# The first store of a rotary-embedding kernel in two requests: 16 partitions, then 112

## The chip, the cores and the metric

The kernel runs on one core of a Trainium2 chip. The time is device microseconds of that core. Before the change it is 318.33 us, the median of three runs (318.25 to 318.38).

The core has engines with instruction streams of their own: VectorE (DVE), GpSimd (POOL), ScalarE (ACT), SyncE (SP) and TensorE (PE, not used here). Sixteen DMA engines move data between the chip's memory (HBM) and the on-chip memory (SBUF, 128 partitions). An engine's instruction stream asks for a transfer, and the DMA engines carry it out; SP's requests and ACT's requests stand in two queues, which the page calls q1 and q10.

## The reference

Rotary position embedding on `x` of shape (8, 2048, 16, 64): batch, position, head, element. The tables `cos` and `sin` have 32 columns for each position.

```
x1 = x[..., :32];  x2 = x[..., 32:]
out1 = x1 * cos - x2 * sin
out2 = x1 * sin + x2 * cos
out  = concatenate([out1, out2], axis=-1)
```

All is float32. The input and the output have 67.1 MB each.

## The kernel before

The 2048 positions of a batch lie on 128 partitions, 16 positions (J) on each. A piece is half of that, 8 positions (R) of one batch, so there are 16 pieces. A piece is 4 MB: 128 partitions with one contiguous run of 32 KB each, in SBUF as in HBM.

The buffer `buf` holds five pieces (NBUF). Piece p is loaded into slot p mod 5 by SP (`load`, line 52), is rotated in place, and is stored from there by ACT (`store`, line 55). The load of piece p + 5 is asked for after the store of piece p and has to wait until that store has landed. The loads of the first five pieces are asked for at the start, that of piece 0 in three parts with the two tables between them. The sixteen pieces make 18 loads of `x`, and, since the last piece is stored in three parts, 18 stores.

`rotate` (line 69) works on some of a piece's positions. VectorE multiplies the halves, swapped, by a sine table with its sign folded in, into a scratch tile `v` (line 80), and then multiplies the piece by the cosine table in place (line 93). GpSimd adds `v` (line 99). Most pieces take two such steps of four positions. In the last piece VectorE does part of the addition itself (lines 87 and 96). ScalarE prepares the tables (lines 108 to 110) and from then on only asks for stores.

The order of VectorE's instructions is fixed by `in_order`. For the rest, each engine follows the program's order, and the tile framework sets the waits: a store waits for the additions of its piece, a load for the store that frees its slot. The framework also gives each transfer one of eight semaphores, in turn; a transfer that takes over a semaphore waits until the transfer that had it before has landed.

The change touches `store` (line 54) and the branch for the first piece in the main loop (line 112), where the whole of piece 0 is stored with one request after three steps of `rotate`.

Of the kernel before, what the change touches and what calls it, by code (L numbers as in the profile page):

```python
# [1 line left out]

# [4 lines left out]


@with_exitstack  # L10
def kernel(
    ctx: ExitStack,
    tc: tile.TileContext,
    x: bass.AP,
    cos: bass.AP,
    sin: bass.AP,
    out: bass.AP,
):
    nc = tc.nc
    f32 = mybir.dt.float32  # L20

    B, S, H, D = x.shape
    Dh = D // 2
    P = nc.NUM_PARTITIONS
    J = S // P
    R = 8
    C = 4
    HALVES = J // R
    NP = B * HALVES
    NBUF = 5  # L30

    const_pool = ctx.enter_context(tc.tile_pool(name="rope_const", bufs=1))
    io_pool = ctx.enter_context(tc.tile_pool(name="rope_io", bufs=1))
    tmp_pool = ctx.enter_context(tc.tile_pool(name="rope_tmp", bufs=2))
    ps_pool = ctx.enter_context(tc.tile_pool(name="rope_ps", bufs=1, space=bass.MemoryType.PSUM))
    psv_pool = ctx.enter_context(tc.tile_pool(name="rope_psv", bufs=1, space=bass.MemoryType.PSUM))

    sin_f = const_pool.tile([P, J, Dh], f32)
    cos_f = const_pool.tile([P, J, Dh], f32)
    sin_p = ps_pool.tile([P, J, D], f32)  # L40
    cos_p = ps_pool.tile([P, J, Dh], f32)
    buf = io_pool.tile([P, NBUF, R, H, D], f32)

    def rows(t, p, r0, r1):
        b, j0 = p // HALVES, (p % HALVES) * R
        return t[b].rearrange("(p j) h d -> p j (h d)", j=J)[:, j0 + r0 : j0 + r1, :].rearrange("p j f -> p (j f)")

    def flat(t):
        return t.rearrange("p j h d -> p (j h d)")

    def load(p, r0=0, r1=R):
        nc.sync.dma_start(out=flat(buf[:, p % NBUF, r0:r1, :, :]), in_=rows(x, p, r0, r1))  # L52

    def store(p, r0=0, r1=R):
        nc.scalar.dma_start(out=rows(out, p, r0, r1), in_=flat(buf[:, p % NBUF, r0:r1, :, :]))

    order = []

    def in_order(op):
        if order:  # L60
            tc.add_manual_dep(
                op.ins,
                order[-1].ins.name,
                mybir.DependencyInfo(mybir.DependencyClass.NoSync, mybir.DependencyReason.DATA),
                reason="order of the vector engine",
            )
        order.append(op)

    def rotate(p, r0, r1, on_vector=0):
        n = r1 - r0  # L70
        j0 = (p % HALVES) * R + r0
        js = slice(j0, j0 + n)
        xt = buf[:, p % NBUF, r0:r1, :, :]
        rev = xt.rearrange("p j h (e d) -> p j h e d", e=2)[:, :, :, ::-1, :]
        sin_b = sin_p[:, js, :].rearrange("p j (e d) -> p j e d", e=2).unsqueeze(2).to_broadcast([P, n, H, 2, Dh])
        cos_b = cos_p[:, js, :].unsqueeze(2).to_broadcast([P, n, 2 * H, Dh])
        m = n - on_vector
        if m:
            v = tmp_pool.tile([P, C, H, D], f32)
            in_order(nc.vector.tensor_mul(  # L80
                out=v[:, 0:m, :, :].rearrange("p j h (e d) -> p j h e d", e=2),
                in0=rev[:, 0:m, :, :, :],
                in1=sin_b[:, 0:m, :, :, :],
            ))
        if on_vector:
            w = psv_pool.tile([P, 2, H, D], f32)
            in_order(nc.vector.tensor_mul(  # L87
                out=w[:, 0:on_vector, :, :].rearrange("p j h (e d) -> p j h e d", e=2),
                in0=rev[:, m:n, :, :, :],
                in1=sin_b[:, m:n, :, :, :],  # L90
            ))
        xw = xt.rearrange("p j h (e d) -> p j (h e) d", d=Dh)
        in_order(nc.vector.tensor_mul(out=xw, in0=xw, in1=cos_b))  # L93
        if on_vector:
            xa = flat(xt[:, m:n, :, :])
            in_order(nc.vector.tensor_add(out=xa, in0=xa, in1=flat(w[:, 0:on_vector, :, :])))  # L96
        if m:
            xa = flat(xt[:, 0:m, :, :])
            nc.gpsimd.tensor_add(out=xa, in0=xa, in1=flat(v[:, 0:m, :, :]))  # L99

    nc.sync.dma_start(out=sin_f, in_=sin.rearrange("(p j) d -> p j d", j=J))  # L101
    load(0, 0, 2)
    nc.sync.dma_start(out=cos_f, in_=cos.rearrange("(p j) d -> p j d", j=J))
    load(0, 2, 4)
    load(0, 4, R)
    for p in range(1, NBUF):
        load(p)
    nc.scalar.copy(out=sin_p[:, :, Dh:D], in_=sin_f)  # L108
    nc.scalar.mul(out=sin_p[:, :, 0:Dh], in_=sin_f, mul=-1.0)  # L109
    nc.scalar.copy(out=cos_p, in_=cos_f)  # L110
    for p in range(NP):
        if p == 0:
            rotate(p, 0, 2)
            rotate(p, 2, 4)
            rotate(p, 4, 8)
            store(p)
        elif p == NP - 1:
            rotate(p, 0, 4, 1)
            store(p, 0, 4)
            rotate(p, 4, 6, 1)  # L120
            store(p, 4, 6)
            rotate(p, 6, 8, 2)
            store(p, 6, 8)
        else:
            rotate(p, 0, 4)
            rotate(p, 4, 8)
            store(p)
        if p + NBUF < NP:
            load(p + NBUF)


# [1 line left out]
_INS = ['x', 'cos', 'sin']  # L133
_OUTS = [((8, 2048, 16, 64), 'float32')]


# [23 lines left out]
```

## Time and profile before

The table is of one profiled execution.

| What | Value |
|---|---|
| time of the profiled execution | 318.49 us |
| span of its instructions and transfers | 316.7 us |
| median of the runs | 318.33 us |
| GpSimd's additions (line 99) | 33, of which 29 on 128x4096 at 8.86 us |
| VectorE's products (lines 80 and 93) | 67, of which 59 on 128x4096 at 4.42 us |
| whole loads and stores of 4 MB | 15 each, median 31.4 us from request to landing |
| first store | asked for at 33.31 us, landed 24.0 us later |
| last arithmetic instruction ends | 306.2 us |

Times are counted from the start of the span. The time of an execution holds 1.8 us around the span. A duration from request to landing holds the time that a transfer stands in its queue behind others. The DMA rows of a profile give, for a stretch of time, the packets and bytes of each queue and the share of 16 engines' time that they took; a packet here is one partition's contiguous run, or a small packet that closes a transfer on an engine.

### The profile page before, as it was taken

To read this page: it belongs to the slowest core of one execution; us is meant where nothing else is said; L and a number is where in the kernel's file an instruction comes from. 1 tells how busy PE (TensorE), PEld (TensorE's weight loads), DVE (VectorE), ACT (ScalarE), POOL (GpSimd) and SP (SyncE) were. 2 spreads that over 40 slices of the span, in tenths; PEclk is the share of its full clock that TensorE was granted. 3 is DMA by queue.
4 is the path that set the end of the run, shared out by engine and by line. 5 is a ranking of instruction groups with operands and counts; after the bars stand their busy time and mean duration, and the time that the engine had idled before them with its cause. 6 is when DMAs were issued, how large, how long until landed. Compare 5 with 4: busy or idle time off the path is not lost.

```text
span 316.7 us, 272 instructions
## 1 busy us (share of the span) xinstructions
DVE 287.5 (91%) x73; ACT 3.1 (1%) x4; POOL 274.8 (87%) x37
## 2 busy tenths in 40 slices
DVE  2999999999999999999999999799697997979960
ACT  3000000000000000000000000000000000000000
POOL 0659999999999999999999999989969899797900
DMA  7999999999999999999999999999999999999997
GB/s 301 460 430 447 348 464 426 435 451 410 459 401 464 397 464 397 464 414 447 435 426 459 401 464 397 464 398 459 410 451 435 426 451 410 455 406 460 406 428 300
DMA packets 5474, 134.76 MB, mean 425 GB/s; under 512 B 608, under 2 KB 608, under 8 KB 864
## 3 DMA queue, kind: packets, MB, share of 16 engines
q1 hardware_dynamic: 2880, 67.63, 50.0%
q10 hardware_dynamic: 2592, 67.11, 49.1%
q14 instruction: 2, 0.02, 0.0%
HBM read 67.63 MB, written 67.11 MB: 425 GB/s over the span
## 4 chain that ended last, share of the span: by engine, by line
POOL 39%; DMA 32%; DVE 21%; issue 3%; SPq 0%; POOLq 0%; DVEq 0%
POOL buf L99 39%; DMA buf<-in_x_dram 22%; DMA out_dram<-buf 11%; DVE buf L93 10%; DVE v L80 8%; DVE buf L96 1%; DVE w L87 1%; SPq L101 0%; POOLq L99 0%; DVEq L80 0%; SPq L52 0%
## 5 line engine op out<-in xcount | busy, mean ns | idle before, releaser
L99 POOL TENSOR_TENSOR buf<-buf,v 128x4096 f32<-128x4096 f32 (+3 forms) x33 | 274.6, 8335 | 26.2 <-DVE buf L93 25.8
L80 DVE TENSOR_TENSOR v<-buf,sin_p 128x4096 f32<-128x4096 f32 (+3 forms) x33 | 137.3, 4161 | 17.3 <-DMA buf<-in_x_dram 15.7
L93 DVE TENSOR_TENSOR buf<-buf,cos_p 128x4096 f32<-128x4096 f32 (+1 forms) x34 | 141.8, 4170 | 1.2
L96 DVE TENSOR_TENSOR buf<-buf,w 128x1024 f32<-128x1024 f32 (+1 forms) x3 | 4.7, 1575 | 0.1
L87 DVE TENSOR_TENSOR w<-buf,sin_p 128x1024 f32<-128x1024 f32 (+1 forms) x3 | 4.7, 1579 | 0.0
L108 ACT ACT_TABLE_LOAD x1 | 1.3, 1283 | 0.7 <-PEq L144 0.7
L110 ACT COPY cos_p<-cos_f 128x512 f32<-128x512 f32 x1 | 0.6, 590 | 2.1 <-DMA cos_f<-in_cos_dram 2.1
L108 ACT COPY sin_p<-sin_f 128x512 f32<-128x512 f32 x1 | 0.6, 589 | 1.4 <-DMA sin_f<-in_sin_dram 1.4
L109 ACT ACTIVATE sin_p<-sin_f 128x512 f32<-128x512 f32 x1 | 0.6, 601 | 0.0
L144 POOL MEMSET const-float32-0.0<- 128x1 f32 x1 | 0.1, 98 | 0.2 <-issue 0.2
L144 POOL MEMSET const-bfloat16-1.0<- 128x1 bf16 x1 | 0.1, 101 | 0.0
L144 POOL MEMSET const-uint8-127<- 128x1 uint8 x1 | 0.1, 101 | 0.0
L144 POOL MEMSET const-float32-1.0<- 128x1 f32 x1 | 0.1, 98 | 0.0
## 6 DMA issues: line engine op xcount, KB each, us to landing
buf<-in_x_dram SPq DMA_DIRECT2D x15, 4096.0 KB, 31.4
out_dram<-buf ACTq DMA_DIRECT2D x15, 4096.0 KB, 31.4
buf<-in_x_dram SPq DMA_DIRECT2D x2, 1024.0 KB, 6.0
buf<-in_x_dram SPq DMA_DIRECT2D x1, 2048.0 KB, 11.5
out_dram<-buf ACTq DMA_DIRECT2D x1, 2048.0 KB, 11.9
out_dram<-buf ACTq DMA_DIRECT2D x2, 1024.0 KB, 10.8
sin_f<-in_sin_dram SPq DMA_DIRECT2D x1, 256.0 KB, 2.7
cos_f<-in_cos_dram SPq DMA_DIRECT2D x1, 256.0 KB, 5.1
```

The lines of the kernel that those rows point to most:

```text
L80: in_order(nc.vector.tensor_mul(out=v[:, 0:m, :, :].rearrange("p j h (e d) -> p j h e d", e=2), in0=rev[:, 0:m, :, :, :], in1=sin_b[:, 0:m ...
L87: in_order(nc.vector.tensor_mul(out=w[:, 0:on_vector, :, :].rearrange("p j h (e d) -> p j h e d", e=2), in0=rev[:, m:n, :, :, :], in1=sin_ ...
L93: in_order(nc.vector.tensor_mul(out=xw, in0=xw, in1=cos_b))
L96: in_order(nc.vector.tensor_add(out=xa, in0=xa, in1=flat(w[:, 0:on_vector, :, :])))
L99: nc.gpsimd.tensor_add(out=xa, in0=xa, in1=flat(v[:, 0:m, :, :]))
L108: nc.scalar.copy(out=sin_p[:, :, Dh:D], in_=sin_f)
L109: nc.scalar.mul(out=sin_p[:, :, 0:Dh], in_=sin_f, mul=-1.0)
L110: nc.scalar.copy(out=cos_p, in_=cos_f)
L144: nc = _bacc.Bacc("TRN2", target_bir_lowering=False, num_devices=1)
```

## The change

`store` gets a range of partitions, all 128 unless told otherwise, and the store of the first piece becomes two requests. The first has partitions 0 to 15, the second, directly behind it in ACT's stream, partitions 16 to 127. Both have all eight positions, 32 KB for each partition: 0.52 MB and 3.67 MB. Together they write what the one request wrote. All other stores, the loads and the arithmetic stay as they are. The later transfers get other semaphores, since one more transfer is counted.

```
-    def store(p, r0=0, r1=R):
-        nc.scalar.dma_start(out=rows(out, p, r0, r1), in_=flat(buf[:, p % NBUF, r0:r1, :, :]))
+    def store(p, r0=0, r1=R, a=0, b=P):
+        nc.scalar.dma_start(out=rows(out, p, r0, r1)[a:b], in_=flat(buf[a:b, p % NBUF, r0:r1, :, :]))
...
             rotate(p, 4, 8)
-            store(p)
+            store(p, 0, R, 0, 16)
+            store(p, 0, R, 16, P)
         elif p == NP - 1:
```

## The prediction

> **What bounds the kernel now.** I read the page first (span, the busy row of the DMA engines, the queues), then the waits, then the last stretch by windows, and only then the place of the change.
>
> ```profile
> span 316.7 us, 272 instructions
> ...
> DVE 287.5 (91%) x73; ACT 3.1 (1%) x4; POOL 274.8 (87%) x37
> ...
> DMA  7999999999999999999999999999999999999997
> ...
> DMA packets 5474, 134.76 MB, mean 425 GB/s; under 512 B 608, under 2 KB 608, under 8 KB 864
> ...
> q1 hardware_dynamic: 2880, 67.63, 50.0%
> q10 hardware_dynamic: 2592, 67.11, 49.1%
> ```
>
> The 16 DMA engines are busy in every slice but the first and the last. q1 carries the loads and q10 the stores, and together they fill 99.1% of 16 engines' span. Each of the 15 whole stores moves 128 rows of 32,768 bytes; 67.11 MB are 2048 such rows' worth of bytes, and 49.1% of 16 x 316.7 us is 2488 us, so a row costs one engine 1.215 us and 16 engines together move one round of 16 rows in that time. The small packets number 608 = 38 transfers x 16: every transfer ends with one small packet on each engine.
>
> ```profile
> DVE v L80 <- DMA buf<-in_x_dram: 15.7, 7, 6.1
> ```
>
> ```profile
> core 0: us, DVE busy (x) ACT busy (x) POOL busy (x), PEclk, DMA share, GB/s
> 283.00:306.20 23.20, 22.78 (x11) 0.00 (x0) 16.48 (x3) 1.00 0.99 426
> 306.20:316.70 10.50, 0.00 (x0) 0.00 (x0) 0.00 (x0) 1.00 0.78 332
> ```
>
> The first line, from the waits, says that VectorE stands still for loads; six of the seven times lie after 180 us. The windows show that after the last arithmetic, at 306.2 us, the DMA still needs 10.5 us. GpSimd is 87% busy, but the work ends when the transfers end. So time in which a DMA engine moves nothing is paid one for one at the end, and a short delay on VectorE or GpSimd is not: they would meet a shorter wait for loads later.
>
> Now the first store, asked for at 33.31 us (windows of time first, then the DMA queues in two of them):
>
> ```profile
> 24.00:33.20 9.20, 9.08 (x3) 0.00 (x0) 8.79 (x1) 1.00 1.06 456
> 35.00:38.38 3.38, 3.35 (x2) 0.00 (x0) 3.38 (x1) 1.00 0.96 310
> 38.38:48.10 9.72, 9.69 (x3) 0.00 (x0) 9.56 (x2) 1.00 1.01 438
> ```
>
> ```profile
> q1 hardware_dynamic: 32, 1.05, 95.9%
> ```
>
> ```profile
> q1 hardware_dynamic: 16, 0.52, 52.7%
> q10 hardware_dynamic: 16, 0.52, 52.7%
> ```
>
> Between 35.0 and 38.38 us the engines count as busy but move 310 GB/s: only two rounds of load rows (the 32 of the first q1 line) in the time of 2.8 rounds, so about 3.38 - 2 x 1.215 = 0.95 us are lost, once, when the store queue starts. The last two lines are the window 38.3 to 40.6 us: from there one round of loads and one of stores take turns, at full rate. I found no stretch like it later.
>
> **The change part by part.** It touches one store of the eighteen. No byte is added: 16 rows and then 112 rows instead of 128.
>
> ```profile
> L55 ACTq DMA_DIRECT2D out_dram<-buf x18: 338/338/377, 33.3 to 306.2; - x18
> ```
>
> ```profile
> q1 hardware_dynamic: 16, 0.00, 0.8%
> ```
>
> One more issue on ACT: 0.34 us. The two parts are asked for at 33.31 and about 33.7 us. Behind them on ACT stands only the second store, asked for at 51.2 us when GpSimd finishes, so 17 us cover it: 0. The second part has a wait of its own, on the semaphore of the first load (asked for at 1.16 us, landed 6.0 us later), passed long before: 0. From there on the transfers' semaphores are dealt out one place further, so most later stores and loads name others in their waits; each names an earlier transfer of its queue or one that it needed anyway. I find none that would be late: 0.
>
> One more set of 16 small packets: the last line above (window 281.6 to 282.7 us) shows 16 of them in 0.8% of 16 x 1.1 us, 0.009 us on each engine. They also take one turn of the store queue, so the loads get one round ahead: 1.2 us of order, no work. Sum 0.01.
>
> The load of the sixth piece on SP now waits for both parts. It was asked for at 57.35 us (the store asked for at 33.31, landing 24.0 later). The fifth load, asked for after the cosine's landing at 6.7 us and 62.7 us on its way, keeps the load queue fed until 69. A store later by a turn and by the 1.7 us found below moves the request to about 60.3: covered by 9 us. Its landing moves from 57.35 + 31.4 = 88.8 to about 91.7, and VectorE first wants it at 95.7: covered by 4. If that cover were gone, VectorE would wait some us, and the loads after it are not late, since the DMA goes on. Behind it on SP stands the next load, which waits for the second store.
>
> What no row shows is a transfer of fewer than 128 partitions. The 16 rows are the first term. From below: one row per engine, the same round as any other, 0 (a gain is treated as a rival). From above: the 16 rows lie side by side, one eighth of the partitions; if those are served as in a whole store, where every engine has 8 of the 128 rows, two engines' paths must pass all 16, 8 rounds: 8 x 1.215 - 1.215 = 8.5 us. Between the ends I take the geometric middle, 2.8 rounds, 3.4 us, 2.2 more than now. Two load rounds (2.4 us) ran ahead of the first store row in the window above and can hide some of it; I count half: **1.1 us**.
>
> The 112 rows are the second term: 7 rows per engine, but not the 7 that the engine had when all 128 were asked for together, so engines can meet at the same rows' place. From below 0, since a round of loads lies between two rounds of stores and a late row can be caught up in it. From above each of 7 rounds doubles, 8.5 us. It is nearest to the alternating rounds of the window 38.3 to 40.6, which run at full rate, so I stay near the lower end, half a round: **0.6 us**.
>
> The sum is 0.01 + 1.1 + 0.6 = 1.7 us. The profiled execution took 318.49 us (span 316.7 and 1.8 around it), 0.16 over the median of 318.33; against it 320.2, against the median **320.0 us**.
>
> A rule stands beside the first term. The row is the 1.215 us per round for rows spread over all partitions. SBUF — State Buffer of the Trainium skill, section "Door 1: The DMA port swizzle", says that a transfer's rate depends on how many of 16 ports its partitions reach, that partitions 0 to 15 reach 4, and gives 104 GB/s measured for them. By that, as an estimate from the page, the 0.52 MB would take 5.0 us, 3.8 more than a round, and the sum would be about 4.4 us with the second term as above. No run here shows it yet.
>
> **The rivals.**
>
> Everything serial, nothing hidden: an engine that waits for a store row does not move load rows meanwhile. Four engines behind each place is then 4 x 1.215 - 1.215 = 3.6 us for the 16 rows, and two collisions among the 7 rounds of the second part add 2.4: 318.33 + 6.0 = 324.3. For it speaks that the load rows slowed down as soon as the first store row was fetched (310 GB/s); against it that two load rounds still passed. The skill's rule just named points this way.
>
> No change: rows of 32 KB go one per engine, collisions drown in the alternating load rounds, and what is left is 0.01 us: 318.4. For it speaks that the bytes per engine are the same and every queue keeps its cover; against it only that the 16 rows lie in one corner.
>
> Faster, the other side: the 0.95 us at the first start of the store queue depends on how much the queue has to offer at once. With a first request of a single row per engine the fetch ahead is shorter, and the loads keep their rate in that window. It decides if the window's rate rises above about 400 GB/s (loss below 0.3 us, a gain above 0.64): 318.33 - 0.95 = 317.4. Against it: the second part comes 0.4 us behind the first, long before the first store row moves at 38.4 us, and the first row is as large as before.
>
> **How the numbers follow.** Slower by 0.6 to 3 us, my forecast, 0.40, own range 319.0 to 321.4, time 320.0. Serial, over 3 us: 0.18. No change: 0.24. Faster: 0.18. A difference under 0.2% (0.64 us) is about what a measurement of this kernel can't tell from none; the three runs shown span 0.13 us. So slower 0.58, same 0.24, faster 0.18. The range runs from the faster rival, 317.4, to 323.6, within the serial one; it leaves out some 0.06 below and 0.12 above.
>
> **What would show it.** In the new profile: two store requests near 33.3 and 33.7 us, 16 more small packets (624), q10 at 67.11 MB. The rate between 35 and about 45 us tells the first term: the same 0.95 us lost means no change, 2 to 3 us lost my forecast, 4 and more the serial case, under 0.3 the faster one. The rate from there to the end of the first store tells the second term: full rate means 0. VectorE's first wait for loads after 180 us should come earlier by what the DMA lost. I am wrong if the difference arises after the first store, for instance from a load request that is late and leaves the load queue empty, or if the engines drift apart and one of them ends late alone.

## The result, and the profile after

The changed kernel takes 323.5 us (median of 6 runs, 321.28 to 325.64), the kernel before 318.53 us beside it (318.25 to 319.73). The ratio is 1.0153, with a 95% interval of 1.0118 to 1.0187: slower by 5.0 us. The time also scatters more: 4.4 us between the ends where the kernel before has 1.5. One run of the changed kernel in a later group (328.45 us) and one of the cut along the positions (323.37 us) count as slow, over 1.5% above the fastest of their group; they are left out of the ratios below, but not of the medians and ranges.

The page of the changed kernel, from one execution of 321.28 us, the fastest of the six:

```profile
span 319.5 us, 277 instructions
...
DVE 287.4 (90%) x73; ACT 3.1 (1%) x4; POOL 274.8 (86%) x37
...
DMA  7999999999999999999999999999999999999996
...
DMA packets 5490, 134.76 MB, mean 422 GB/s; under 512 B 624, under 2 KB 624, under 8 KB 880
...
q1 hardware_dynamic: 2880, 67.63, 49.6%
q10 hardware_dynamic: 2608, 67.11, 49.2%
```

The bytes are the same, the arithmetic takes the same time, and the DMA engines are busy to the end as before. There are 16 more small packets. What changed is the mean rate, 422 GB/s where it was 425, and, as the experiments show, how far apart the sixteen engines end.

The same three windows around the first store:

```profile
24.00:33.20 9.20, 8.98 (x4) 0.00 (x0) 9.04 (x2) 1.00 1.06 456
35.00:38.38 3.38, 3.35 (x2) 0.00 (x0) 3.38 (x1) 1.00 1.48 417
38.38:48.10 9.72, 9.69 (x3) 0.00 (x0) 9.55 (x2) 1.00 0.85 361
```

The low rate has moved: before it was the 3.38 us when the store queue starts, now the 9.72 us after them run at 361 GB/s instead of 438. (A packet is counted where it begins, so long packets make the share of one window exceed 1 and the next fall short.)

The queues between 35 and 41 us, first of the kernel before and then of the changed one, tell whose packets are long:

```profile
q1 hardware_dynamic: 48, 1.57, 74.3%
q10 hardware_dynamic: 29, 0.95, 36.6%
```

```profile
q1 hardware_dynamic: 41, 1.34, 59.8%
q10 hardware_dynamic: 19, 0.52, 43.1%
```

Before, 29 store rows took 36.6% of 16 engines' 6 us, 1.21 us each. Now 16 store rows (and three small packets) take 43.1%, 2.59 us each. In the two later profiles of this kernel it is 3.69 and 3.28 us.

### The profile page after: what moved, and what is told of

The parts are those of the page before. It is cut to its first block, busy times and chain, and to the rows that moved or that the text cites. A ratio compares the mean times of both kernels' runs of the same rounds, so it can differ in the third digit from the quotient of the medians.

```text
span 319.5 us, 277 instructions
## 1 busy us (share of the span) xinstructions
DVE 287.4 (90%) x73; ACT 3.1 (1%) x4; POOL 274.8 (86%) x37
## 4 chain that ended last, share of the span: by engine, by line
DMA 53%; POOL 28%; DVE 13%; issue 3%; SPq 0%; POOLq 0%; DVEq 0%
DMA buf<-in_x_dram 30%; POOL buf L99 28%; DMA out_dram<-buf 22%; DVE buf L93 5%; DVE v L80 4%; DVE buf L96 1%; DVE w L87 1%; SPq L101 0%; POOLq L99 0%; DVEq L80 0%; SPq L52 0%
```

## The experiments

All differences are against the kernel before, run beside each kernel on the same chip.

**The changed kernel again, and a cut that leaves every row in its place.** No edit in the first. The second:

```
-            store(p, 0, R, 0, 16)
-            store(p, 0, R, 16, P)
+            store(p, 0, 1)
+            store(p, 1, R)
```

> The changed kernel once more, beside the kernel before on the same chip. Theory A (place): the 16 neighbouring partitions lie behind few paths into SBUF, 16 engines crowd there, and the first rows of the first store take 2 to 3.5 us each instead of 1.2; the time is 3 to 6 us over the kernel before, as it was. Theory B (two requests): any first store in two requests costs this. Theory C (out of step): the rows lost at the first store are only the trigger; what is paid is that the engines, no longer in step, end at different times, and the distance between the first and the last closing packet of a transfer grows from the first store to the end. A and B say a distance that stays as it is after the first store.

> The first store in two requests cut along the positions: position 0 of all 128 partitions (0.52 MB, as much as the 16 rows), then positions 1 to 7. Theory A: every row stays on its own engine's path, so within 0.5 us of the kernel before. Theory B: 3 to 6 us slower, like the changed kernel. Theory C: like A, since nothing puts the engines out of step. If a smaller first row shortens the slow stretch at the start of the store queue, up to 0.95 us faster.

The changed kernel took 327.45 us against 318.5 (ratio 1.0286, interval 1.0257 to 1.0316): 9.0 us slower here, more than at first and more than any theory gave. The cut along the positions took 320.62 (318.24 to 323.37 in ten runs; 1.0049, interval 1.0022 to 1.0076), 2.1 us slower, with some runs at no cost at all. So two requests as such don't cost 5 to 9 us. But the small cost was not clean either: position 0 is ready after the first step of `rotate`, and its store was asked for at 15.5 us, not at 33.3. A store running through the first loads was a second difference, and a later run takes it away.

The closing packets of a transfer, one per engine, tell how far the engines are apart. In the kernel before, those of the load of piece 3 lie within 0.4 us and those of the last load within 1.0. In this run of the changed kernel it is 2.9 us at piece 3 and 7.5 at the last load; in the cut along positions 1.9 and 4.4. The distance grows, as theory C has it. It grows in the cut along positions too, though all 128 partitions are in each part. (A distance of up to one round, 1.2 us, can be only the turn in which loads and stores alternate.)

**Sixteen rows alone, neighbours or spread.** The second request is gone; in the second kernel the 16 partitions are taken 8 apart.

```
             store(p, 0, R, 0, 16)
-            store(p, 0, R, 16, P)
```

```
-            store(p, 0, R, 0, 16)
-            store(p, 0, R, 16, P)
+            store(p, 0, R, 0, P, 8)
```

(`store` has a sixth argument in the second one, the step from partition to partition.)

> Left out: the second request, so 112 rows of the first piece are never written; the DMA has 7 rounds less, 8.5 us. Theory A: 16 neighbouring partitions alone cost 2 to 3.5 us, so 5 to 6.5 us faster than before. Theory B: no second request, so the full 8.5 us faster. Theory C: the trigger is in the first request, so the engines are out of step to the end and 3 to 6 us remain of the cost: 2.5 to 5.5 us faster.

> Left out as in the run beside it, but the 16 rows that are written are partitions 0, 8, 16 to 120. Theory A: rows from all over SBUF crowd less (some pairs at most), so 0 to 1.2 us of cost: 7.3 to 8.5 us faster than before, and clearly faster than the run with 16 neighbours. If place does not matter, the same as that run. Theory C: faster than that run by what the engines stay nearer in step.

The queues between 35 and 41 us, first with 16 neighbours, then with 16 spread rows:

```profile
q10 hardware_dynamic: 16, 0.52, 63.0%
q1 hardware_dynamic: 32, 1.05, 41.0%
```

```profile
q1 hardware_dynamic: 56, 1.84, 85.2%
q10 hardware_dynamic: 19, 0.52, 20.2%
```

Sixteen neighbours take 3.78 us each (63.0% of 96 us, over 16), 3.1 times a row's usual time, on all engines. Sixteen rows spread over the partitions take 1.21 us each, as in a whole store. The number of bytes, of rows and of rows per engine is the same: where the rows lie is what slows them. In the spread kernel VectorE stands still while its 16 rows move, as the next lines show; but the rows of the whole store take 1.21 us with VectorE busy, so that is not what makes the difference.

With the neighbours the kernel took 311.91 us, 6.6 us less than before. 8.5 us of work are gone, so the 16 rows cost 1.9 us. That is 0.1 us beyond what place alone was given, and it excludes the theory that the trigger alone brings the drift: its 2.5 to 5.5 us are missed, and the engines are 1.0 us apart at piece 3 and 1.4 at the end (2.2 for two loads between, a round's turn, then 1.0 again).

The total of the spread kernel, 322.45 us, says nothing on the rows. The waits show why:

```profile
DVE buf L93 <- DMA out_dram<-buf: 13.6, 1, 13.6
```

VectorE stood 13.6 us for a store. In its program the cosine product of piece 1 waits for the store of piece 0, which it does in no other kernel here; I read this as the framework counting the neighbouring slot as touched when partitions are taken 8 apart. All else came later by that; only the duration of the rows can be used.

**The other part alone, the position cut at the same time, and the cut at a later piece**, with the changed kernel beside them. The 112 rows alone:

```
-            store(p, 0, R, 0, 16)
             store(p, 0, R, 16, P)
```

The cut along the positions with the last position first, which is ready only with the whole piece:

```
-            store(p, 0, R, 0, 16)
-            store(p, 0, R, 16, P)
+            store(p, 7, R)
+            store(p, 0, 7)
```

The first store whole again, and the cut in the branch of the middle pieces:

```
             rotate(p, 4, 8)
-            store(p)
+            if p == 6:
+                store(p, 0, R, 0, 16)
+                store(p, 0, R, 16, P)
+            else:
+                store(p)
```

> The changed kernel a third time, as the measure for the other runs on the same chip: 3 to 9 us slower than the kernel before.

> Left out: the first request, so partitions 0 to 15 of the first piece are never written; the DMA has one round less, 1.2 us. The run with the 16 rows alone kept its engines in step after the first store (1 us apart to the end) and paid 1.9 us for its rows. Theory D: the 112 rows, seven to an engine and on other paths than in a whole store, put the engines out of step, and out of step the load rows are slowed again and again; then this run is slower than the kernel before in spite of the round less, by 1 to 5 us, with engines 3 us or more apart at the end. Theory A without D (only the 16 rows cost): 1.2 us faster, engines in step.

> Two requests again, cut along the positions with all 128 partitions in each, but the last position first, so that both are asked for at 33.3 us as in the changed kernel (position 0 alone was asked for some 9 us earlier). Theory D: every row is on its own engine's path, the engines stay in step, within 0.4 us of the kernel before and engines 1 us apart at the end. If any uneven start of the store queue is enough to bring drift, 1 to 3 us slower with engines 3 us or more apart, as in the run with position 0 first (2.1 us slower).

> The cut into 16 and 112 partitions at the store of piece 6, near 140 us, instead of the first. The 16 rows crowd as before (about 2 us on every engine, perhaps less of it hidden or more, as the store queue is not just starting). Theory D: drift has 175 us left instead of 280, so the part over 2 us is some six tenths of that of the changed kernel: 3 to 6 us slower. If the cost is all paid at the cut itself: the same as the changed kernel. If it needs the start of the store queue: within 0.5 us of the kernel before.

| Kernel | us | ratio to before, 95% interval | engines apart: load of piece 3, last load |
|---|---|---|---|
| before | 318.49 | | 0.4, 1.0 us (first profile) |
| changed | 324.95 | 1.0181, 1.0144 to 1.0219 | 2.9, 7.0 us |
| 112 rows only | 320.89 | 1.0070, 1.0045 to 1.0095 | 2.0, 5.6 us |
| positions, same time | 318.49 | 0.9999, 0.9988 to 1.0009 | 0.3, 1.0 us |
| piece 6 cut | 323.01 | 1.0146, 1.0111 to 1.0181 | 1.1, 6.8 us |

The 112 rows alone are 2.4 us slower with a round less to move: they cost 3.6 us. That is theory D, and the larger part of the change. The queue q10 in two windows that hold the same number of store rows, of the kernel before from 45 to 58 us and of the 112 rows alone from 45 to 60 us, shows the cost of a row:

```profile
q10 hardware_dynamic: 110, 3.08, 54.9%
```

```profile
q10 hardware_dynamic: 110, 3.08, 52.8%
```

Both lines hold 94 rows and 16 small packets. The rows take 1.21 us each before and 1.35 on average now: in the records of single packets 15 of the 112 rows take more than 1.23 us, the longest 3.11, and none of 128 before. That is 0.8 us per engine as a mean, but it falls unevenly, and the closing packets of that first store lie 4.65 us apart. An uneven number of rows is not the reason: followed back from its closing packet, through packets that begin where another ends, each of the sixteen engines has seven. The slow rows in the part that I had priced at half a round drive the engines apart at once. The two parts measured alone add up to 5.5 us; the change as a whole cost 5.0, 9.0 and 6.5 us in its three groups of runs.

The cut along the positions, with both requests at the same time, is the same as the kernel before to 0.1%. So the second request, its waits and its 16 small packets cost nothing, and with every row in its usual place and no earlier start the engines stay in step.

The cut at piece 6 costs 4.5 us, seven tenths of the 6.5 us that the cut at piece 0 cost on that chip (eight tenths by the ratios). It does not need the start of the store queue. In that run the engines were 1.1 us apart in every load up to piece 8, and the next was at 3.3.

What being out of step does at the end can be read in windows, of the kernel before and of the changed one of this group (span 324.0 us); the last two numbers are the share of the 16 engines and GB/s:

```profile
306.00:312.00 6.00, 0.18 (x1) 0.00 (x0) 0.00 (x0) 1.00 0.98 418
312.00:314.00 2.00, 0.00 (x0) 0.00 (x0) 0.00 (x0) 1.00 1.03 434
314.00:316.00 2.00, 0.00 (x0) 0.00 (x0) 0.00 (x0) 1.00 0.24 98
```

```profile
316.00:318.00 2.00, 0.00 (x0) 0.00 (x0) 0.00 (x0) 1.00 0.58 246
318.00:320.00 2.00, 0.00 (x0) 0.00 (x0) 0.00 (x0) 1.00 0.17 74
320.00:322.00 2.00, 0.00 (x0) 0.00 (x0) 0.00 (x0) 1.00 0.11 45
322.00:324.00 2.00, 0.00 (x0) 0.00 (x0) 0.00 (x0) 1.00 0.02 8
```

Before, all engines work to 314 us and are done within the next 1.4. After, from 318 us on 0.17 of the engines' time, three of sixteen, is in use, and the kernel waits five microseconds for these few.

Between the cut and the end a second thing is at work. In windows from 60 to 280 us the kernel before and the changed one of this group read:

```profile
60.00:140.00 80.00, 79.10 (x19) 0.00 (x0) 79.21 (x9) 1.00 1.00 433
140.00:220.00 80.00, 77.13 (x19) 0.00 (x0) 77.36 (x10) 1.00 1.01 436
220.00:280.00 60.00, 53.97 (x13) 0.00 (x0) 54.16 (x7) 1.00 1.00 433
```

```profile
60.00:140.00 80.00, 79.09 (x19) 0.00 (x0) 79.17 (x9) 1.00 1.00 431
140.00:220.00 80.00, 72.20 (x18) 0.00 (x0) 72.45 (x10) 1.00 1.00 430
220.00:280.00 60.00, 53.42 (x13) 0.00 (x0) 53.63 (x7) 1.00 1.00 430
```

All transfers here are whole ones, 128 partitions each. Still 430 GB/s stand against 433 to 436. In the records of single packets the kernel before has one load row over 1.23 us between 60 and 260 us; this one has 119 (up to 1.88 us) and seven store rows where it had three. Load rows are slowed now and then once the engines are apart. How often differs: the first profile of the changed kernel has 55 such load rows and 433 GB/s from 60 to 280 us, where this one has 430 and the kernel before 434.

**Halves, and the cut when the loads are over.**

```
-            store(p, 0, R, 0, 16)
-            store(p, 0, R, 16, P)
+            store(p, 0, R, 0, 64)
+            store(p, 0, R, 64, P)
```

The second kernel is that of piece 6 with another number:

```
-            if p == 6:
+            if p == 14:
```

> The first store in two halves, partitions 0 to 63 and 64 to 127, four rows per engine in each. If crowding goes by how many engines share the place of neighbouring rows, the halves crowd less than 16 neighbours (rows of up to 2.4 us, not 3.8) and some engines read on their usual paths: 0.5 to 3 us slower than the kernel before, less than with 16 and 112. If any cut along the partitions puts the engines out of step in the same way, as much as with 16 and 112: 5 to 9 us. If only neighbours among 16 rows count: no change.

> The cut into 16 and 112 partitions at the store of piece 14, asked for near 282 us, when the last load is just landing. Theory D as read so far: the drift after the cut is load rows that are slowed while the engines are out of step; with no load rows left only the cut itself is paid, on the slowest engine: 1.5 to 3.5 us slower than the kernel before. If drift grows among stores too: 4 us or more. If a store queue with a backlog hides the 16 rows: under 1 us.

The halves took 324.33 us against 318.6 (1.0176, interval 1.0119 to 1.0234), 5.7 us slower: no less than 16 and 112. My dose by neighbours is refuted (the longest store row also took 3.07 us, not 2.4), and the second guess, as much from any cut along the partitions, holds for the two cuts tried. In the profiled execution (322.35 us, the fastest of four) the store was 6 us apart at once, 57.7 to 63.9 us, and then nothing grew: 3.3 us from the load of piece 4 to the last. In this execution the cut alone made the cost. The others of the four reach 326.61.

The cut at piece 14 took 326.97 us (1.0255, interval 1.023 to 1.028), 8.4 us slower. I had expected 1.5 to 3.5, or 4 and more if drift grows among stores too; the number falls under the second, but most of the cost arises in the cut store itself. Windows of the kernel before, then of this one:

```profile
294.00:306.00 12.00, 11.83 (x7) 0.00 (x0) 7.23 (x2) 1.00 0.96 412
306.00:312.00 6.00, 0.18 (x1) 0.00 (x0) 0.00 (x0) 1.00 0.98 418
```

```profile
294.00:306.00 12.00, 11.28 (x6) 0.00 (x0) 6.51 (x2) 1.00 1.01 306
306.00:312.00 6.00, 0.00 (x0) 0.00 (x0) 0.00 (x0) 1.00 0.93 295
```

The engines are busy all along and move 306 and 295 GB/s. The 128 rows of this store are too long by 4.8 us per engine, against 1.5 to 2.7 us in the first store of the changed kernel's three profiles and 1.6 us in the cut at piece 6. My reading is that among stores alone the crowded rows follow each other, and no load round lies between two of them in which an engine could do something else. If so, the alternation with loads, on which I had placed the second term, does hide something; it hides less than I gave it. The times alone don't show it: 8.4 us lies within the 5.0 to 9.0 of the cut at the first store.

## Why the prediction was right or wrong

The direction was right, and 323.5 us lies in the range, 0.1 us below its upper end. That is partly luck: the two later groups of the same kernel, at 327.45 and 324.95 us, lie above the range, and a cost of over 3 us had a chance of only 0.18. The time of the forecast, 320.0, is 3.5 us short. One term was a little short, and one failed.

**What bounds the kernel**: right, with a correction. A lost microsecond of the DMA was to be paid one for one. It is, if every engine loses it: with the 16 rows alone store and load rows took 2.6 us too long per engine where the kernel before loses 0.8, and 1.9 us were paid. If engines lose different amounts, the one that lost most is paid, and mean rates hide it.

**The second request, its waits, the small packets**: right at 0. There are 624 small packets, and the position cut at the same time, with as many requests, is at 0.9999.

**The load of the sixth piece** was to move to about 60.3 us and stay covered. It was asked for at 60.46 in the changed kernel, and after its very first load VectorE waited 0.2 us for loads up to 160 us. Between 160 and 180 us it waited 1.8 us, where the kernel before waits first at 185: earlier, as it was to be, but by some 17 us and not by the few that the DMA had lost. (The first load, said to have landed 6.0 us after its request, landed 4.9 us after it, at 6.0; nothing hangs on it.)

**The first term**, the 16 rows: 2.8 rounds were taken, part hidden, 1.1 us. Alone, the rows took 3.1 rounds and cost 1.9 us. Mechanism right, size short by 0.8. What is hidden is the 0.8 us that load rows lose in the kernel before and do not lose in that run. The sign that I had named, 2 to 3 us lost between 35 and 45 us, came true: from 33 to 48 us the load and store rows in the three profiles of the changed kernel are too long by 2.0, 2.6 and 2.4 us per engine. By SBUF — State Buffer of the Trainium skill, section "Door 1: The DMA port swizzle", partitions 0 to 15 reach 4 of 16 ports; as an estimate from that, four rounds of 1.21 us. The trace has 3.1, so the direction agrees. By the same port map of the Trainium skill the 16 spread partitions reach 8 ports, which would be two rounds by the same estimate; the trace has 1.0, so there it does not agree. That the missing part was fetched ahead, before the packet is counted as begun, is my guess.

**The second term**, the 112 rows: this is the step that failed. Half a round, 0.6 us, was taken, near the lower end, because loads and stores alternate and a late row could be caught up. It measured 3.6 us. Two things were wrong in it: the alternation hides too little, and I had counted one common delay for all engines where they are driven apart, by 4.65 us in one store. As a mean over the engines the slow store rows are only 0.8 us, near my 0.6; the kernel pays for the engine that is last. The test that I had named for this term, the rate until the end of the first store, could hardly show it: from 48 to 64 us the rows in the three profiles of the changed kernel are too long by 0.4 us per engine at most. (The upper end that I named, 8.5 us for seven doubled rounds, is near the 8.4 us of the cut among stores alone; that is chance, since those are for both parts.)

**The rivals.** No change and faster are out for the cut along the partitions. For the cut along the positions no change is what was measured, and the 0.95 us at the start of the store queue stayed, 1.0 us in its load rows: a smaller first row does not take it away. The serial rival, 324.3 us, is nearer to the runs (323.5, 327.45, 324.95) than my forecast. Its sum fits, its parts don't: 3.6 and 2.4 us for what measured 1.9 and 3.6, since it too had one delay for all engines in the second part.

**What would make it wrong** named the engines drifting apart with one ending late alone, and had no price for it. It belonged in the sum, since the trace of before already shows one engine, alone, 0.6 us late at the end after an instruction fetch at 210 us.

The section "Can I just issue two DMAs to hit both halves?" of the Trainium skill's page SBUF — State Buffer says that two transfers on the two halves serialize and that a single transfer over all partitions is the only way to reach all ports. The halves here, 1.8% slower than the whole store, agree that the single transfer is the better one; their two requests stand in one queue, so no run here shows the serializing itself.

What stays open is why load rows are slowed once the engines are apart, why the distance grows in some executions (2.9 to 7.0 us) and stays in others (3.3 us with the halves), and why the same kernel cost 5.0, 9.0 and 6.5 us in three groups. No run separates the memory's side from the transfers' own.

## What to carry to other kernels

When transfers fill the whole span, cut a transfer along its contiguous run and leave all 128 partitions in each part: that cost nothing here with both parts asked for together, and 2.1 us with one part asked for 18 us earlier, while a cut along the partitions, of one store in eighteen, cost 4.5 to 9 us. Judge such a change by the slowest DMA engine, so look at the closing packets and at the share of engines busy in the last microseconds, and not only at mean GB/s. The same cut crowded its rows more among stores alone (4.8 us too long per engine) than beside loads (1.5 to 2.7).

## What the runs showed of the hardware

- A row of 32 KB takes an engine 1.21 us. Sixteen neighbouring partitions, one row on each engine, took 3.78 us each when stored alone and 2.59 to 3.69 with the other 112 behind them; sixteen partitions 8 apart took 1.21.
- Sixteen engines in step stay in step: 0.4 us apart at piece 3, 1.0 at the end. One store cut along the partitions puts them 3 to 6 us apart and nothing brings them back in 280 us. A small store of all 128 partitions, asked for at 15.5 us among the first loads, was followed by 1.9 us at piece 3 and 4.4 at the end.
- Out of step, whole transfers from 60 to 280 us ran at 433, 431 and 430 GB/s in three profiles of the changed kernel, against 434 before, through load rows of up to 2.0 us; and the time of an execution scatters, 321.3 to 328.9 us over all runs of the changed kernel, where the kernel before stays within 318.2 to 319.9.
